# A hybrid decoder layer on one core: half of the opening's row of c by a broadcast load, the first x on ScalarE's queue, and the order planned anew

## Chip, core and metric

The kernel runs on one core of a Trainium2 chip. The metric is the device time of one execution in microseconds (us), shown as the median of several runs. A profiled execution has a time of its own, and its span runs from the first instruction to the last.

## What is computed

One layer over 1024 tokens with a model width of 1024, in f32. Cut to what matters:

```python
c_act = jax.nn.silu(c)
mod = c_act @ mod_w[l] + mod_b[l]
shift, scale, gate = jnp.split(mod, 3, axis=-1)
h = rmsnorm(x, norm_g[l]) * (1.0 + scale[:, None, :]) + shift[:, None, :]
u = h @ w_in[l]
cv, cg, cs, lx, ls = jnp.split(u, [...], axis=-1)
v = cv * jax.nn.sigmoid(cg)
v = causal_depthwise_conv(v, dw_w[l], dw_b[l])          # 31 taps
v = jax.nn.silu(layernorm(v, cln_g[l], cln_b[l])) @ pw2_w[l] + pw2_b[l]
y_conv = v * jax.nn.silu(cs)
xs = causal_depthwise_conv(lx, sc_w[l], sc_b[l])        # 4 taps
r = sigmoid(per-head xs @ wr + br);  i = sigmoid(per-head xs @ wi + bi)
a = exp(-8 r softplus(-lam))
hs = scan of h = a h + sqrt(1 - a^2) (i xs)
y_lru = hs * jax.nn.silu(ls)
x = x + (1.0 + gate[:, None, :]) * (jnp.concatenate([y_conv, y_lru], axis=-1) @ w_out[l])
return rmsnorm(x, final_g)
```

The modulation needs silu(c), a vector of 1024, multiplied into each of 3072 rows of mod_w (which the host hands over turned, so that a row lies in a partition).

## The kernel before

Data lie with channels in the 128 partitions and tokens along the free axis, so a tensor of 1024 by 1024 is eight tiles of 128 by 1024. Every f32 product is made of three passes on TensorE: an operand is cast to a shorter type ("hi", on ScalarE), the remainder ("lo") is formed by a subtraction on VectorE or GpSimd or by an accumulating DMA, and hi by hi, lo by hi and hi by lo are added in PSUM.

Stages, in order: the opening; the input products (forty column blocks of w_in, `slots`, some of them in pairs that save a part of the products, `duo`); the gates and scans of the recurrent group, whose heads are the `g` entries among the slots; the recurrent half of the output products (`lru_pair`); the layer norm of the conv group; its pointwise products (`pw2`); the other half of the output products, with the closing norm and the stores.

The opening (lines 1825 to 2032) does not wait for the norm of x. Its first products, `first`, take four column blocks of w_in and x scaled by `gs = (1 + scale) * norm_g` alone; the norm of a token is multiplied in afterwards. So the first product needs the first eighth of `gs`, which needs a dot product of silu(c) with 128 rows of mod_w. For it silu(c) must lie as a row in every partition:

- V, all the small vectors, is loaded first (line 1483); c lies in it as a column per block, 128 by 8. ScalarE makes `cs` of it (line 1834).
- TensorE spreads `cs` into a row in all partitions: per block one product of the column, broadcast along the free axis, with the identity (`spread_c`, lines 1843 to 1846). There are two halves of four blocks, each in a PSUM tile of its own, `c_row0` and `c_row1`. Each product in f32 shows as two MATMUL instructions, so sixteen in all.
- VectorE takes the dot of each half with the first block of mod_w (`first_dot`, lines 1938 to 1950). The two halves are added through the bias `b1`; then `gs` (line 1961), the scaled x `uh` (line 1973), and the first product can start.
- ScalarE copies the halves of the row to SBUF as `sc` for the later dots.

TensorE fills its time before that with idle products of ones, twelve of them (`IDLE`), four ahead of the spread and eight behind it. ScalarE also makes exp(-|lam|) there (`sp_u`, lines 1836 and 1837) and loads the table for the square root (line 1838), so that three tables are loaded one after the other in the first six microseconds.

Loads are issued by SyncE (SP) in the order of `LOADS`: the first block of mod_w ("s0"), the first weights ("w0"), the first half of x ("a0") and its second ("b0"), and then for each further block mod_w, weights and x. The first x tile comes in two halves of 256 KB, the halves of its columns (`x_load`, lines 1859 to 1866).

The order of all instructions is planned by the program itself before it emits anything (`Plan.order`, from line 1224). Each operation has an engine, an estimated cost and a priority; the planner simulates the engines and lets each take, of the operations that are ready, the one with the lowest priority number. A load is ready to be read some fixed time after its issue. The table `TURNS` adds small corrections to the priorities of single operations, some nine hundred of them. `ORDER` is the list of the column blocks and gates behind the opening.

Of the kernel before, what the change touches and what calls it, by code (L numbers as in the profile page):

```python
# [9 lines left out]
F32 = mybir.dt.float32  # L10
# [4 lines left out]
P = 128  # L15
# [19 lines left out]
ORDER = "i10 i24 i2 g0 i25 i11 i3 i26 i33 i12 i4 g1 i34 i23 g2 i13 i35 i5 i27 g3 i20 i39 i14 i6 i28+i36 i15 i30+i37 i7 i29+i38 g6 g4 g5 i31 i19 i22+i18 g7 i21"  # L35
# [55 lines left out]
KQ = 0.5  # L91
# [9 lines left out]
DENG = {14: ("POOL", "DMA", "DVE"), 17: ("POOL", "DVE", "DVE"), 20: ("DVE", "DVE", "DMA"), 21: ("DMA", "DMA", "DVE"), 24: ("DMA", "DVE", "POOL"), 26: ("DVE", "DMA", "DMA"), 27: ("POOL", "DMA", "POOL"), 30: ("DVE", "DVE", "DVE"), 35: ("DMA", "POOL", "DVE"), 36: ("POOL", "POOL", "POOL"), 39: ("DVE", "DVE", "POOL"), 40: ("DVE", "DVE", "DMA")}  # L101
# [7 lines left out]
LTP = 0.0  # L109
# [13 lines left out]
XADDP = -1.5  # L123
TSRC = "POOL"
HSP = -60
# [3 lines left out]
CENG = {21: "POOL", 17: "DVE", 36: "DVE", 33: "POOL", 22: "POOL", 15: "POOL", 16: "DVE", 27: "POOL", 20: "POOL", 31: "POOL", 34: "POOL", 24: "POOL", 29: "POOL", 38: "POOL", 39: "DVE", 32: "POOL"}  # L129
# [7 lines left out]
SQADD = -1.0  # L137
BEHIND0 = 2
# [39 lines left out]
PDIRECT = (4,)  # L178
D1S = {15: -1.35, 17: -1.35, 18: -1.35, 19: 0.0, 20: -1.35, 21: -0.3, 22: 0.0, 23: -1.35, 25: -1.35, 26: -1.35, 29: -0.3, 32: -1.35, 33: -0.3, 35: -1.35, 36: -1.35, 38: -1.35, 39: -0.3, 40: 0.0, 41: -1.35}
# [22 lines left out]
    ("ACT", "c1", "cq1_11", 0): 1.2,  # L202
    ("ACT", "c1", "cq1_12", 0): -7,
    ("ACT", "c1", "cq1_13", 0): -2.2,
    ("ACT", "c1", "cq1_14", 0): -5,
    ("ACT", "c1", "cq1_15", 0): 2,
# [5 lines left out]
    ("ACT", "c3", "c3", 0): 6.4,  # L212
    ("ACT", "c3", "cq3_1", 0): 5.6,
    ("ACT", "c3", "cq3_10", 0): 1.7,
    ("ACT", "c3", "cq3_11", 0): 5.9,
    ("ACT", "c3", "cq3_12", 0): 1.4,
    ("ACT", "c3", "cq3_13", 0): 8,
    ("ACT", "c3", "cq3_14", 0): 0.2,
    ("ACT", "c3", "cq3_2", 0): 2,
    ("ACT", "c3", "cq3_3", 0): 4.8,  # L220
    ("ACT", "c3", "cq3_4", 0): 1.4,
    ("ACT", "c3", "cq3_5", 0): 0.3,
    ("ACT", "c3", "cq3_6", 0): 3.3,
    ("ACT", "c3", "cq3_7", 0): 5.7,
    ("ACT", "c3", "cq3_8", 0): 6.7,
    ("ACT", "c3", "cq3_9", 0): 1.7,
    ("ACT", "c3", "es3", 0): 2.8,
    ("ACT", "c3", "lnsq3", 0): 0.2,
    ("ACT", "c5", "lnsq5", 0): 0.1,
    ("ACT", "c6", "caccs6", 0): -1.6,  # L230
    ("ACT", "c6", "vha3", 0): 2,
    ("ACT", "c7", "c7", 0): -0.1,
    ("ACT", "c7", "caccs7", 0): 1,
    ("ACT", "c7", "vhb3", 0): -2.3,
    ("ACT", "cacc2", "c2", 0): -0.1,
    ("ACT", "cacc6", "c6", 0): -0.7,
    ("ACT", "caccs7", "c7", 0): -0.7,
# [6 lines left out]
    ("ACT", "cr4", "cr4", 0): 7.9,  # L244
    ("ACT", "cr4", "vha2", 0): 6.4,
    ("ACT", "dn37", "wk37", 0): -1.6,
    ("ACT", "first_u0", "first_u0", 0): 8.1,
    ("ACT", "fraw2", "fhi2", 0): -1,
# [8 lines left out]
    ("ACT", "gate6_1", "g6", 0): 0.1,  # L257
    ("ACT", "graw6", "ghi6", 0): 0.1,
# [5 lines left out]
    ("ACT", "lh3", "ll3", 0): -4,  # L264
# [8 lines left out]
    ("ACT", "next5", "scs0", 0): -0.1,  # L273
    ("ACT", "ps13", "xs2", 0): 0.1,
    ("ACT", "ps17", "sls2", 0): -2,
    ("ACT", "ps18", "scs7", 0): -8,
# [3 lines left out]
    ("ACT", "psbias", "psbias", 0): -4,  # L280
# [8 lines left out]
    ("ACT", "r7", "r7", 0): -1.2,  # L289
    ("ACT", "r7", "r7", 1): -3.2,  # L290
# [3 lines left out]
    ("ACT", "raw27", "whi27", 0): 0.1,  # L294
    ("ACT", "raw34", "whi34", 0): -0.1,
    ("ACT", "raw35", "whi35", 0): -0.1,
    ("ACT", "raw36", "whi36", 0): -2.4,
    ("ACT", "raw38", "whi38", 0): -0.1,
# [4 lines left out]
    ("ACT", "rawout0_1", "h34out0", 0): 1.9,  # L303
    ("ACT", "rawout0_1", "hlout0", 0): 2,
    ("ACT", "rawpw20_1", "h34pw20", 0): 0.1,
    ("ACT", "rawpw21_0", "whipw21", 0): 0.7,
    ("ACT", "rawpw22_1", "h34pw22", 0): 1,
# [24 lines left out]
    ("ACT", "v1", "cq1_9", 0): -1,  # L332
# [12 lines left out]
    ("ACT", "v3", "cq3_1", 0): 1.6,  # L345
# [5 lines left out]
    ("ACT", "v3", "cq3_4", 0): 1.8,  # L351
    ("ACT", "v3", "cq3_5", 0): -0.1,
    ("ACT", "v3", "cq3_6", 0): 1.8,
# [10 lines left out]
    ("ACT", "vt1", "vhc1", 0): -0.1,  # L364
# [4 lines left out]
    ("ACT", "whi32", "wlo32", 0): -0.1,  # L369
    ("ACT", "whipw20", "wlopw20", 0): -2,  # L370
    ("ACT", "wz37", "wsh37", 0): -1.9,
    ("ACT", "x0", "uh0", 1): -0.1,
    ("ACT", "x2", "uh2", 0): 4,
    ("ACT", "x3", "uh3", 2): -0.9,
    ("ACT", "x4", "uh4", 2): 0.1,
# [7 lines left out]
    ("ACT", "x7", "uh7", 1): 0.3,  # L383
    ("ACT", "xpw2_1", "yc2", 1): -0.3,
    ("ACT", "xs4", "xsh4", 0): 0.1,
# [6 lines left out]
    ("ACT", "yh4", "yl4", 0): -5.7,  # L392
    ("ACT", "yhc0", "ylc0", 0): 0.9,
    ("ACT", "yhc1", "ylc1", 0): 1,
# [7 lines left out]
    ("DVE", "a1", "r1", 1): 0.4,  # L402
    ("DVE", "a4", "r4", 1): 1,
    ("DVE", "a6", "r6", 1): 0.3,
    ("DVE", "a7", "r7", 0): -0.1,
    ("DVE", "acc0", "lp0", 1): -0.3,
# [13 lines left out]
    ("DVE", "c2", "caccs2", 11): -0.1,  # L420
# [11 lines left out]
    ("DVE", "c4", "caccs4", 8): 0.1,  # L432
# [3 lines left out]
    ("DVE", "c4", "caccs4", 13): -0.2,  # L436
# [11 lines left out]
    ("DVE", "c5", "caccs5", 12): -0.2,  # L448
    ("DVE", "c5", "caccs5", 13): -0.1,
    ("DVE", "c5", "caccs5", 14): 2.9,  # L450
    ("DVE", "c5", "caccs5", 15): -3.8,
    ("DVE", "c5", "caccs5", 16): 1.3,
    ("DVE", "c5", "lnwide", 0): -0.5,
    ("DVE", "c5", "mean", 0): -1.5,
    ("DVE", "c5", "vlb2", 0): 2.1,
    ("DVE", "c5", "vt2", 1): 1.6,
    ("DVE", "c5", "vu2", 0): 8.9,
    ("DVE", "c6", "cacc6", 0): -0.6,
    ("DVE", "c6", "caccs6", 2): 1,
    ("DVE", "c6", "caccs6", 4): -0.5,  # L460
    ("DVE", "c6", "caccs6", 6): 2,
# [2624 lines left out]
```

## Time and profile before

| | |
|---|---|
| runs shown | 721.14, 722.94, 723.27 us; median 722.94 us |
| the profiled execution | 722.46 us, of which the span is 720.6 us |
| TensorE busy | 710.4 us, 99% of the span |
| VectorE busy | 641.5 us, 89% |
| ScalarE busy | 477.3 us, 66% |
| GpSimd busy | 218.2 us, 30% |
| granted TensorE clock, mean | 0.997 |
| moved by DMA | 137.53 MB, 191 GB/s |

In the rows that follow, PE is TensorE's matrix multiply, DVE VectorE, ACT ScalarE, POOL GpSimd and SPq the queue of SyncE. A row of the timeline gives the start in us from the span's start, the duration in us, engine, line, operation, the tiles written and read (buffer numbers left out), the shape and the count; in brackets stands the engine's idle time before it and what ended that. A row of a wait gives the engine with the tile, what it waited for, the total in us, how often, and the longest. Times of matmuls are start to end, and matmuls overlap, so that the distance between starts is what one costs.

### The profile page before, as it was taken

The page shows a single profiled execution, that of the slowest core. Times are in us where ns is not written, and L with a number is a line of the kernel's source. Part 1 is how long each engine was busy: PE and PEld are TensorE (multiplying, and loading weights), DVE is VectorE, ACT ScalarE, POOL GpSimd, SP SyncE. Part 2 cuts the span into 40 slices and gives each one's busy share as a digit, 9 for nine tenths or more (in the row PEclk, how much of TensorE's full clock was granted, in tenths as well). Part 3 has the DMA queues.
Part 4 walks back from the last instruction along what each step waited for, and adds up shares of the span by engine and source line. Part 5 has one row for each costly group of instructions (what it writes and reads, how often), then busy time and mean ns, then how long its engine had stood idle before and what let it go on. Part 6 is the DMA issues. An engine that isn't in the chain of part 4 may idle for free.

```text
span 720.6 us, 9035 instructions
## 1 busy us (share of the span) xinstructions
PE 710.4 (99%) x3230; PEld 590.3 (82%) x3230; DVE 641.5 (89%) x885; ACT 477.3 (66%) x604; POOL 218.2 (30%) x188
## 2 busy tenths in 40 slices
PE   9999999999999999999999999999999999999995
PEld 8888888888888888888888888887887888878885
DVE  7989999799999989969988998998589976998747
ACT  7651598847857874974794979937589653744422
POOL 0022434543676752474162351100102100100001
PEclk9999999999999999999999999999999999999998
DMA  9935458999697999699664339999638755892006
GB/s 341 407 154 176 73 149 204 246 270 204 119 253 187 250 240 229 169 230 206 211 176 117 88 98 282 264 301 246 161 81 204 183 124 123 239 279 93 27 1 233
DMA packets 45500, 137.53 MB, mean 191 GB/s; under 512 B 5144, under 2 KB 14624, under 8 KB 45344
## 3 DMA queue, kind: packets, MB, share of 16 engines
q0 software_dynamic: 16848, 45.52, 35.2%
q1 hardware_dynamic: 27600, 90.53, 35.1%
q10 hardware_dynamic: 1008, 0.92, 0.4%
q8 instruction: 25, 0.41, 0.2%
q14 instruction: 19, 0.16, 0.1%
HBM read 84.22 MB, written 25.69 MB: 153 GB/s over the span
## 4 chain that ended last, share of the span: by engine, by line
PE 78%; DVE 10%; ACT 4%; issue 4%; DMA 3%; POOL 1%; DVEq 0%; POOLq 0%; ACTq 0%
PE ps L1575 34%; PE xpw L1751 6%; PE xout L1751 6%; PE first L1884 5%; PE dn L2713 3%; PE ypw L1751 3%; PE gate L2315 3%; PE dn L1575 3%; DVE caccs L1434 2%; PE up L1575 2%; PE lx L2468 2%; PE y L1721 1%; DMA wlo<-in_w_out_dram 1%; DMA wloout<-in_w_out_dram 1%; PE zpw L1751 1%
## 5 line engine op out<-in xcount | busy, mean ns | idle before, releaser
L1575 PE MATMUL ps<-uh,whi 128*128 128x512 f32 x448 | 138.0, 389 | 0.0
L1575 PE MATMUL ps<-uh,wlo 128*128 128x512 f32 x448 | 137.9, 389 | 0.0
L1575 PE MATMUL ps<-ul,whi 128*128 128x512 f32 x448 | 137.9, 389 | 0.0
L1575 PEld LDWEIGHTS ps<-uh,wlo 128*128 128x128 f32 x448 | 84.1, 188 | 17.5
L1575 PEld LDWEIGHTS ps<-ul,whi 128*128 128x128 f32 x448 | 84.1, 188 | 17.4
L1575 PEld LDWEIGHTS ps<-uh,whi 128*128 128x128 f32 x448 | 84.0, 188 | 17.4
L1434 DVE SCALAR_TENSOR_TENSOR cacc<-v,V,cacc 128x511 f32<-128x511 f32 (+14 forms) x90 | 66.5, 739 | 0.3
L1434 DVE SCALAR_TENSOR_TENSOR caccs<-v,V,caccs 128x511 f32<-128x511 f32 (+6 forms) x84 | 62.4, 743 | 1.0
L1434 DVE SCALAR_TENSOR_TENSOR caccs<-c,wsum,caccs 128x511 f32<-128x511 f32 (+6 forms) x84 | 62.2, 740 | 0.8
L1415 ACT CAST whi<-raw 128x1024 fp32r<-128x1024 f32 (+1 forms) x44 | 44.1, 1006 | 26.7 <-issue 14.0
L1423 ACT ACT_TABLE_LOAD x46 | 59.0, 1283 | 3.2 <-DVE r L2327 1.1
L1442 POOL TENSOR_TENSOR wlo<-raw,whi 128x1024 fp32r<-128x1024 f32 (+1 forms) x15 | 36.4, 2428 | 75.5 <-ACT whi L1415 73.5
L1447 POOL DMA_DIRECT2D es<-cq x30 | 28.3, 943 | 32.1 <-DMA es<-cq 11.1
L1434 DVE SCALAR_TENSOR_TENSOR modw<-modw,sc 128x1024 f32<-128x1024 f32 x23 | 32.7, 1425 | 0.0
L1442 DVE TENSOR_TENSOR wlo<-raw,whi 128x1024 fp32r<-128x1024 f32 (+1 forms) x22 | 30.7, 1395 | 0.6 <-ACT whi L1415 0.6
L1447 POOL DMA_DIRECT2D oo<-co x26 | 26.5, 1054 | 11.1 <-issue 5.5
L1423 ACT ACTIVATE uh<-x,shift 128x512 fp32r<-128x512 f32 x16 | 10.5, 713 | 23.9 <-PE ps L1575 23.9
L1442 POOL TENSOR_TENSOR o<-fin,bc 128x256 f32<-128x256 f32 (+1 forms) x6 | 4.9, 831 | 70.8 <-ACT bc L1415 70.8
L1447 POOL DMA_DIRECT2D accd<-acc x8 | 7.3, 914 | 62.1 <-ACT acc L1423 44.2
L1423 ACT ACTIVATE finsq<-fin 128x512 f32<-128x512 f32 (+2 forms) x14 | 7.9, 570 | 27.0 <-DVE fin L1434 15.1
L1423 ACT ACTIVATE cq<-v,V 128x511 f32<-128x511 f32 (+14 forms) x30 | 21.0, 707 | 6.5 <-DVE r L2327 3.1
L1447 POOL DMA_DIRECT2D lz<-in_w_out_dram x16 | 14.4, 987 | 34.4 <-ACT lz L1423 30.5
(525 smaller groups left out, 1937.8 us busy)
## 6 DMA issues: line engine op xcount, KB each, us to landing
raw<-in_w_in_dram SPq DMA_DIRECT2D x36, 512.0 KB, 4.6
modw<-in_mod_w_dram SPq DMA_DIRECT2D x24, 512.0 KB, 7.6
scsd<-scs SPq DMA_DIRECT2D x8, 512.0 KB, 3.9
raw<-in_w_out_dram SPq DMA_DIRECT2D x8, 512.0 KB, 4.5
accd<-acc POOLq DMA_DIRECT2D x8, 512.0 KB, 8.0
rawpw<-in_pw_dram SPq DMA_DIRECT2D x8, 512.0 KB, 3.9
scsr<-scsd SPq DMA_DIRECT2D x8, 512.0 KB, 4.3
rawout<-in_w_out_dram SPq DMA_DIRECT2D x8, 512.0 KB, 4.4
```

The lines of the kernel that those rows point to most:

```text
L1415: act.copy(out(), in_())
L1423: act.activation(out=out(), in_=in_(), func=func, **kw)
L1434: dve.scalar_tensor_tensor(out=out(), in0=in0(), scalar=scalar, in1=in1(), op0=op0, op1=op1, accum_out=accum)
L1442: lambda: e.tensor_tensor(out=out(), in0=a(), in1=b(), op=op), prio, r, w,
L1447: return S.op("POOL", ISSUE, lambda: pool.dma_start(out(), a(), accum_op=ALU.add), prio, r, w, lag=RATE * n / T, after=after, flight=flight)
L1575: pe.matmul(ps()[:, a - off:b - off], k3(lhs)()[:, at, :], rhs[k]()[:, a:b], start=(k == first and lhs is wh and rhs is xh and (a - off) % ...
L1721: pe.matmul(to(), half(*lhs)()[:, j * P:j * P + P], half(*rhs)()[:, c0:c1], start=a == "S1" and j == 0 and t == 0, stop=j == KT // 2 - 1 a ...
L1751: pe.matmul(half(ps, 0)(), half(*lhs)()[:, j * P:j * P + P], half(*rhs)(), start=start and at == 0 and i == 0, stop=at == len(order) - 1 a ...
L1884: pe.matmul(ps()[:, a - off:b - off], fw_part(lhs, k, i * P, i * P + P)(), rhs()[:, a:b], start=k == 0 and lhs is wh and rhs is xh, stop=k ...
L2315: pe.matmul(ps()[:, c0:c1], lhs()[:, j, :], rhs()[:, c0:c1], start=st == 0, stop=st == 2)
L2468: pe.matmul(half(ps, h)(), lhs()[:, o:o + P], half(*rhs)(), start=begin and at == 0 and t == 0, stop=at == len(order) - 1 and t == len(ter ...
L2713: pe.matmul(half(ps, h)(), lhs()[:, o:o + P], half(rhs, z)(), start=begin and j == 0 and t == 0, stop=j == NJ - 1 and t == 2, skip_group_c ...
```

## The change

In the opening:

- The column of c is loaded by itself, ahead of V, and `cs` is made of it.
- Only the first half of the row is spread by TensorE, four blocks instead of eight, into one PSUM tile. The second half comes as a new input, `c_half`, by a load that broadcasts 512 values to all partitions, issued on SP ahead of the first block of mod_w; ScalarE applies silu to it in place.
- The first dot takes the loaded half, the second the spread half. One copy to SBUF is left.
- exp(-|lam|) is made behind the silu of the loaded half, and the table for the square root is loaded behind the seventh scaled x.
- The first half of the first x tile is issued by ScalarE and not by SP.
- The idle products read one column of ones, broadcast, and not a full tile.

In the planner's inputs: two pairs of neighbours in `ORDER` change places (g6 with g4; g7 with i21), the priorities `KQ` (the casts of the pairs' sums), `LTP` (the sums of the recurrent group) and some others change, and several hundred entries of `TURNS` are new, gone or different. The entries of `DENG`, `CENG` and `D1S` count only at the numbers of pairs (27, 30, 33, 37); at those only an entry that equals the default is added. The output lies in memory as 128 rows of 8192 values, and the host puts it back; a store still writes rows of 1 or 2 KB. `SQE` and `OPAIR` are empty.

```diff
-ORDER = "... i29+i38 g6 g4 g5 i31 i19 i22+i18 g7 i21"
+ORDER = "... i29+i38 g4 g6 g5 i31 i19 i22+i18 i21 g7"
...
-KQ = 0.5
+KQ = -0.3
...
-LTP = 0.0
+LTP = -0.5
...
+CRP, EXPP, SQK, SCP = -100.6, -100.3, 6, -98.9
...
+    c_col = const.tile([P, KT], F32, tag="c_col", name="c_col")
+    sp.dma_start(c_col, vecs[:, OFF["c"]:OFF["c"] + KT])
     V = const.tile([P, NVEC], F32, tag="V", name="V")
     sp.dma_start(V[:, :DWW], vecs[:, :DWW])
...
+    one = const.tile([P, 1], F32, tag="one", name="one")
+    dve.memset(one, 1.0)
...
-    cs, ps_c = ctile("cs", KT), [mm_tile(f"c_row{z}") for z in (0, 1)]
-    ACT(-130, lambda: cs, lambda: V[:, OFF["c"]:OFF["c"] + KT], AF.Silu, KT, w=[("cs", 0)])
+    cs, ps_c = ctile("cs", KT), mm_tile("c_row")
+    ACT(-130, lambda: cs, lambda: c_col, AF.Silu, KT, w=[("cs", 0)])
     sp_u = S.buf("sp_u", "sp_u")
-    ACT(-129, sp_u, lambda: V[:, OFF["lam"]:OFF["lam"] + KT], AF.Abs, KT, w=[sp_u])
-    ACT(-128, sp_u, sp_u, AF.Exp, KT, scale=-1.0, r=[sp_u, ("cs", 0)], w=[sp_u])
-    ACT(-127, lambda: junk, lambda: eps_t, AF.Sqrt, 1, r=[sp_u], w=[("junk", 0)])
...
-        pe.matmul(psb()[:, :P], ones, ones, start=True, stop=True)
...
+        pe.matmul(psb()[:, :P], one.to_broadcast([P, P]), one.to_broadcast([P, P]), start=True, stop=True)
+
+    def spread_c():
+        for k in range(KT // 2):
+            pe.matmul(ps_c()[:, k * P:k * P + P], cs[:, k:k + 1].to_broadcast([P, P]), ident,
                       start=True, stop=True)
...
+        elif z == 0:
+            S.op("ACT", 0.05, lambda: act.dma_start(half(t, z)(), xT[:P // 2, :].rearrange(
+                "r (h f) -> (r h) f", h=2)), -140, [], halves(t, 0, H), moved=0.73)
...
+    DMA(CRP, half(sc, 1), lambda: c_half.to_broadcast([P, H]), FULL_BYTES // 2, w=[(sc, 1)])
+    silu_row = ACT(CRP, half(sc, 1), half(sc, 1), AF.Silu, H, r=[(sc, 1)], w=[(sc, 1)])
+    ACT(EXPP, sp_u, lambda: V[:, OFF["lam"]:OFF["lam"] + KT], AF.Abs, KT, w=[sp_u], after=[silu_row])
+    ACT(EXPP, sp_u, sp_u, AF.Exp, KT, scale=-1.0, r=[sp_u, ("cs", 0)], w=[sp_u])
...
-        parts = ((0, H, a0, ("a0", 0)), (H, T, col(macc, j), ("macc", j)))
-        for z, (a, e, to, key) in enumerate(parts):
-            o = STT(p, part(m, a, e), part(m, a, e), 1.0, half(ps_c[z], 0), ALU.mult, ALU.mult, H,
-                accum=to, r=[(m, z), ps_c[z]], w=[(m, z), key])
-            ACT(-101, half(sc, z), half(ps_c[z], 0), "copy", H, r=[ps_c[z]], w=[(sc, z)],
-                after=[o])
-            if z == 0:
+        for z, to, key in ((1, a0, ("a0", 0)), (0, col(macc, j), ("macc", j))):
+            row, rk = (half(sc, 1), (sc, 1)) if z else (half(ps_c, 0), (ps_c, 0))
+            m_ = part(m, z * H, z * H + H)
+            o = STT(p, m_, m_, 1.0, row, ALU.mult, ALU.mult, H, accum=to, r=[(m, z), rk], w=[(m, z), key],
+                    after=[] if z else [o])
+            if z:
                 S.op("DVE", 0.2, lambda: dve.tensor_tensor(
                     out=col(b1, 0), in0=a0, in1=col(b1, 0), op=ALU.add), p,
                     [("a0", 0), ("b1", 0)], [("b1", 0)], lock=True)
+        ACT(SCP, half(sc, 0), half(ps_c, 0), "copy", H, r=[(ps_c, 0)], w=[(sc, 0)], after=[o])
...
+        if k == SQK:
+            ACT(p, lambda: junk, lambda: eps_t, AF.Sqrt, 1, r=[sp_u], w=[("junk", 0)], after=[o])
```

More of the change, by code (lines that the diff above doesn't have):

```diff
@@ L517 @@
     ("DVE", "lnss", "lnsq5", 0): -1,
+    ("DVE", "lx1", "ld1", 0): 0.1,
     ("DVE", "lx3", "ld3", 0): -1,
@@ L1810, in rstd @@
                       after=after if k == 0 else [])
-            for _ in range(warm[k] if warm else 0):
+            for _ in range(warm[k] if k < len(warm) else 0):
                 S.op("PE", 0.22, warm_mm, prio, [], [idle], after=[at], columns=4 * P)
```

529 lines of the change are left out of this document (260 added, 269 removed).

## The prediction

> **What bounds the kernel now.** I read the page's engine table first, then the chain of waits, then what TensorE waited for, then the opening instruction by instruction.
>
> ```profile
> span 720.6 us, 9035 instructions
> PE 710.4 (99%) x3230; PEld 590.3 (82%) x3230; DVE 641.5 (89%) x885; ACT 477.3 (66%) x604; POOL 218.2 (30%) x188
> ```
>
> TensorE (PE) is busy for 710.4 of 720.6 us. "Busy" is modelled, so I check it against the chain, where groups of matmuls stand with their counts:
>
> ```profile
> 3.14 3.63 PE c_row L1845 x16
> 6.77 1.90 PE token_stats L1841 x16
> 8.67 32.68 PE first L1884 x144
> ```
>
> The 144 matmuls of `first` take 32.68 us, 0.227 us each, with no gap. So the kernel is TensorE work end to end, with a head before the first product, a few waits, and a tail of scaling and stores after the last product. What TensorE waited for:
>
> ```profile
> PE lw L1575 <- DMA wlo<-in_w_out_dram: 0.8, 1, 0.8
> PE zout L1751 <- DMA wloout<-in_w_out_dram: 0.6, 1, 0.6
> PE finbc L1798 <- ACT finsqz L1423: 0.3, 1, 0.3
> PE xpw L1751 <- ACT vha L1415: 0.2, 1, 0.2
> ```
>
> One more wait is hidden in a pair of matmuls of the recurrent group's first products:
>
> ```profile
> 466.62 1.03 PE L2468 MATMUL ly<-yls,lsh 128*128 128x512 f32 x2
> 467.49 0.40 PE L1575 MATMUL dn<-uh,whi 128*128 128x512 f32 x1
> ```
>
> Two matmuls that should take 0.45 us hold the engine for 0.87 (466.62 to 467.49): 0.4 us lost. Everything that a new order can win inside is thus 0.8 + 0.6 + 0.2 + 0.4 = 2.0 us; the 0.3 belongs to the closing norm. The rest must come from the head.
>
> The head, in the timeline of the opening:
>
> ```profile
> 0.74 1.28 ACT L1423 ACT_TABLE_LOAD   x1 [0.74 <-PEq L3078]
> 0.75 0.39 SPq L1483 DMA_DIRECT2D V<-in_vecs_dram  x1
> 1.06 2.07 PE L1841 MATMUL token_stats<-ones 128*128 128x128 f32 x8 [1.06 <-DVE ones L1492]
> 1.20 0.42 SPq L1461 DMA_DIRECT2D modw<-in_mod_w_dram  x1
> 2.13 0.91 SPq L1461 DMA_DIRECT2D x<-in_xT_dram  x2
> 2.67 0.21 ACT L1423 ACTIVATE cs<-V 128x8 f32<-128x8 f32 x1 [0.64 <-DMA V<-in_vecs_dram]
> 3.02 3.75 PE L1845 MATMUL c_row<-ident,cs 128*128 128x128 f32 x16
> 5.10 0.69 DVE L1434 SCALAR_TENSOR_TENSOR modw<-modw,c_row 128x512 f32<-128x512 f32 x1 [2.19 <-PE c_row L1845]
> 5.83 0.16 DVE L1948 TENSOR_TENSOR b<-a,b 128x1 f32<-128x1 f32 x1
> 6.38 0.62 ACT L1415 CAST fhi<-fraw 128x512 fp32r<-128x512 f32 x1
> 6.56 2.11 PE L1841 MATMUL token_stats<-ones 128*128 128x128 f32 x16
> 6.81 0.69 DVE L1434 SCALAR_TENSOR_TENSOR modw<-modw,c_row 128x512 f32<-128x512 f32 x1 [0.82 <-PE c_row L1845]
> 7.54 0.22 DVE L1961 SCALAR_TENSOR_TENSOR gs<-macc,b,V 128x1 f32<-128x1 f32 x1
> 7.79 0.49 DVE L1456 TENSOR_SCALAR uh<-x,gs 128x512 fp32r<-128x512 f32 x1
> 8.43 1.17 PE L1884 MATMUL first<-uh,fhi 128*128 128x512 f32 x4
> ```
>
> The chain is V landing, silu of c (2.67), sixteen spread matmuls (3.02 to 6.77), two half dot products on VectorE (5.10 and 6.81, both released by `c_row`), `gs`, `uh`, first product at 8.43. The second dot could have started right behind the add, at 5.83 + 0.16 = 5.99; it waited 0.82 us for the second half of the spread.
>
> **The change part by part.** The spread matmuls fall from sixteen to eight. That takes 1.9 us (8 x 3.75/16) from TensorE's opening, but none of it was product work, and the eight idle matmul pairs behind them still stand in the queue. With dots back to back, the first product follows the start of the first dot by 5.99 - 5.10 = 0.9 and then by 8.43 - 6.81 = 1.62: 2.5 us. If the first dot still began at 5.10, the first product would come at 7.6, a gain of 0.8. But what the first dot now waits for is no longer `c_row`; it is the block of mod_w, and the row's half with its silu. These come from transfers:
>
> ```profile
> modw<-in_mod_w_dram SPq DMA_DIRECT2D x1, 512.0 KB, 3.6
> modw<-in_mod_w_dram SPq DMA_DIRECT2D x24, 512.0 KB, 7.6
> lnwide<-lnrow SPq DMA_DIRECT2D x1, 512.0 KB, 5.8
> 0.00:3.00 3.00, 1.94 (x8) 1.79 (x9) 0.77 (x5) 1.60 (x4) 0.70 (x6) 1.00 0.37 116
> 3.00:6.00 3.00, 3.00 (x15) 3.00 (x15) 0.85 (x3) 2.96 (x5) 0.00 (x0) 1.00 0.91 296
> 9.00:12.00 3.00, 3.00 (x15) 2.46 (x14) 3.00 (x6) 1.80 (x3) 0.00 (x0) 1.00 1.03 420
> ```
>
> (The first three: KB and median us from issue to landing, the first of them for the opening's first block alone; the last three end in the DMA engines' busy share and GB/s.) Before, mod_w lands at 1.20 + 3.6 = 4.8, just ahead of 5.10. After, SP issues the c column, V and the broadcast half ahead of it; SP's issues stand 0.46 us apart (0.75, 1.20), so mod_w is issued at 2.13 and, with the same 3.6 us, lands at 5.7. By bytes: V, x's first half, the broadcast and mod_w are 1,122 kB, where before V and mod_w were 598 kB. The windows moved 348 kB by 3.0 us and then 296 GB/s, so 598 kB are through at 3.85, and landing is told 0.95 later. 1,122 kB are through at 5.6: landing at 6.55, the **upper end**. At 420 GB/s behind 3.0, and with the x half (262 kB, 0.6 us at that rate) hidden in the slow first window, it is 3.0 + 1.84 + 0.95 - 0.6 = 5.2, the **lower end**. I take the issue's 5.7, which lies between. First product: 5.7 + 2.5 = 8.2, a gain of **0.2 us** (0.7 won to 0.65 lost).
>
> A page of the Trainium skill speaks against the move of x: "DMA: Bandwidth & Descriptors", "Issuing engines are not separate DMA queues", says that transfers started from several engines share the same 16 DMA engines, so that only issue time is saved. By that rule alone the upper end holds and the opening loses 0.65; no run here has yet shown a transfer from ScalarE in the opening.
>
> The broadcast reads one row 128 times. The trace has one like it, `lnwide<-lnrow`: 512 KB in 5.8 us, between the 3.6 and the 7.6 of the mod_w blocks of that size, so I price it as ordinary. By bytes the half row lands where mod_w did, 4.8, and its silu (0.6 us, as the cast of 128x512) is done at 5.5, under cover of mod_w's 5.7. Queued behind it on ScalarE stand the exp table (1.28), Abs and Exp (0.2 each, as `cs`) and then `fhi`: done at 5.5 + 1.7 + 0.62 = 7.8, against 8.2 where it is needed. The cover is 0.4 us; if the row is later than that, `fhi` sets the start. x issued by ScalarE ahead of its table load costs nothing: 0.4 (as SP's issues) + 1.28 from 0.74 ends at 2.4, before the c column lands (V's 2.67 or a little sooner). The sqrt table load moves behind k = 6, where ScalarE has room.
>
> Next along: 256 KB more (0.6 us at 420 GB/s) stand ahead of the second block.
>
> ```profile
> 11.27 0.22 DVE L1961 SCALAR_TENSOR_TENSOR gs<-macc,b,V 128x1 f32<-128x1 f32 x1
> 11.52 1.34 ACT L1423 ACTIVATE uh<-x,gs 128x512 fp32r<-128x512 f32 x2 [1.18 <-DVE gs L1961]
> 13.31 0.39 PE L1884 MATMUL first<-uh,fhi 128*128 128x512 f32 x1
> ```
>
> Its first half `uh` is ready near 11.52 + 0.67 = 12.2 and used from about 13.3; 0.6 later still fits a start 0.2 earlier, with 0.3 to spare.
>
> The planner's part: LTP from 0.0 to -0.5 puts the recurrent group's sums ahead of other VectorE work, and those sums (`yls`) are what the 0.4 us at 466.62 waited for. I count that 0.4 as won (0 to 0.4). The transfers behind the waits of 0.8 and 0.6 are touched only by small priorities; I leave both. In ORDER, g7 and i21 change places, which needs a look:
>
> ```profile
> 441.24 0.62 PE L2315 MATMUL gate<-xsh,ghi 128*128 128x512 f32 x2
> 462.59 0.87 POOL L1447 DMA_DIRECT2D yl<-sls  x1 [4.75 <-ACT yl L1423]
> yl<-sls POOLq DMA_DIRECT2D x1, 512.0 KB, 6.6
> 471.36 0.61 PE L1575 MATMUL lp<-yl,whi 128*128 128x512 f32 x2
> 474.08 0.61 PE L1575 MATMUL lp<-yl,whi 128*128 128x512 f32 x2
> ```
>
> Head 7's gate at 441.24 leads to its `yl` landing at 462.59 + 6.6 = 469.2; `lp` reads it at 471.36 at the earliest and at 474.08 at the latest (the first and the last of three such groups; the rows don't tell the heads apart). i21 is 48 matmuls, 10.9 us. I take 0 for the swap in the sum, since the same matmuls of i21 now fill the gaps that the gate filled, and the pair has other products that do not read head 7; the other end is the rival below. The table entries for slot numbers that are no pair, the new layout of the output (rows of the same length) and the new unused options cost nothing.
>
> The sum, against the profiled execution's own 722.46 (span 720.6 and 1.9 around it): 722.46 - 0.2 - 0.4 = **721.9**. That execution is 0.5 below the median of the runs shown, 722.94.
>
> **The rivals.** *The waits go too*: the new order clears 0.8, 0.6 and 0.2 as well, and the opening is at its best: 722.46 - 2.0 - 0.7 = 719.8. For it: the waits are isolated, each on one late transfer or cast. Against: a new order can make new ones as easily. *Head 7 late*: with g7 behind i21, `yl` is 10.9 us later, less the slack of 2.1 to 4.8: 6.1 to 8.8 us of wait in the first pair if nothing else can be drawn forward, 0 if all can; with half of the larger, 4.0, and no gain at `yls`, 722.46 - 0.2 + 4.0 = 726.3, slower. It decides when the gate's second half runs more than 4.8 us later than 441.24 without other products of the pair going ahead. *The opening does not do what it says*: mod_w at 6.55 or the row's silu behind it puts the first product at 9.1: 722.46 + 0.65 = 723.1.
>
> The skill's "TensorE: Matmul & The Clock Gate", Part 1, says that the clock rises after some 3.4 us of work, on a window that runs free of the kernel. The trace agrees that it rises (idle matmuls take 0.26 us at 1.06, 0.13 at 6.56). In an execution where it rose before the spread, the second half would not have held the dots, and the change would win nothing there: that is the third rival again.
>
> **How the numbers follow.** Forecast 0.58, waits gone 0.21, head 7 late 0.12, opening worse 0.09. The bound of 0.3% is 2.2 us, about what a measurement of this kernel can tell from no change. Against 722.94, the forecast and the third rival lie within it, the first lies past 720.8, the second past 725.1: faster 0.21, same 0.67, slower 0.12. The range reaches to the waits-gone case less the closing norm's 0.3 (719.5) and part of the way to head 7 late (724.6, a wait of 2.3); what lies outside is most of head 7 late and the edge of the first rival. The likeliest's own is 721.4 (opening at its best) to 723.1 (at its worst, and `yls` unchanged).
>
> **What would show it.** Right: dots back to back, the first released by a transfer of mod_w, first product between 7.7 and 8.5; no 0.87 us pair on `yls`. Wrong: the first dot waiting for the row's silu, a gap among the `first` matmuls near 13 us, or waits of `lp`, `lx` or `ly` for `yl` of several us. What would make the forecast wrong is waits of more than 2 us, new or gone, in the recurrent or output stages.

## The result and the profile after

The changed kernel takes 726.95 us in the median of nine runs (724.36 to 730.14), the kernel before, on the same chip, 722.07 (720.84 to 726.23). The ratio is 1.0061, with a 95% interval of 1.0039 to 1.0082: it is slower by 0.6%, and the prediction (721.9, no change) was wrong. (Ratios here are estimated from all the runs of both kernels and are not the quotient of the two medians.) The profiled execution took 728.77 us. From its page, the span and TensorE's row:

```profile
span 727.0 us, 9030 instructions
PE 712.1 (98%) x3222; PEld 591.5 (81%) x3222; DVE 643.4 (88%) x886; ACT 477.0 (66%) x604; POOL 217.7 (30%) x188
```

The span is 6.4 us longer than before. TensorE's busy time grew by 1.7, although the opening has eight spread products less (1.9 us): TensorE stands still for longer, and for part of the time it works more slowly. What it waited for in the changed kernel (total, times, longest):

```profile
PE zout L1740 <- DMA wloout<-in_w_out_dram: 2.3, 1, 2.3
PE first L1870 <- DVE uh L1441: 2.1, 1, 2.1
PE lw L1564 <- DMA wlo<-in_w_out_dram: 1.0, 1, 1.0
...
PE dn L2705 <- DVE dn L1427: 0.7, 1, 0.7
```

Before, the first of these was 0.6, the second was not there, the third 0.8, the fourth not there. The two large ones lie at the two ends of the kernel, one in the part that was rebuilt (the opening), one in a part that only the planner touched. The opening of the changed kernel, in the timeline:

```profile
2.13 0.43 SPq L1446 DMA_DIRECT2D modw<-in_mod_w_dram  x1
...
3.41 0.21 ACT L1408 ACTIVATE cs<-c_col 128x8 f32<-128x8 f32 x1 [0.95 <-DMA c_col<-in_vecs_dram]
...
6.05 0.63 ACT L1408 ACTIVATE sc<-sc 128x512 f32<-128x512 f32 x1 [2.43 <-DMA sc<-in_c_half_dram]
...
7.85 0.69 DVE L1419 SCALAR_TENSOR_TENSOR modw<-modw,sc 128x512 f32<-128x512 f32 x1 [3.69 <-DMA modw<-in_mod_w_dram]
...
8.44 0.62 ACT L1400 CAST fhi<-fraw 128x512 fp32r<-128x512 f32 x1
...
8.66 0.68 DVE L1419 SCALAR_TENSOR_TENSOR modw<-modw,c_row 128x512 f32<-128x512 f32 x1
...
9.64 0.49 DVE L1441 TENSOR_SCALAR uh<-x,gs 128x512 fp32r<-128x512 f32 x1
...
10.27 1.10 PE L1870 MATMUL first<-uh,fhi 128*128 128x512 f32 x2 [2.07 <-DVE uh L1441]
```

The chain has the shape that was meant: the two dots stand back to back (7.85 and 8.66), released by a transfer of mod_w. But the transfer is late, and the first product starts at 10.27, where before it started at 8.43. The loads issued in the first 2.5 us (KB, median us from issue to landing):

```profile
modw<-in_mod_w_dram SPq DMA_DIRECT2D x1, 512.0 KB, 5.6
x<-in_xT_dram ACTq DMA_DIRECT2D x1, 256.0 KB, 3.0
sc<-in_c_half_dram SPq DMA_DIRECT2D x1, 256.0 KB, 4.4
```

mod_w lands at 2.13 + 5.6 = 7.7; before it was 4.8. Four windows of the same trace (us; busy us of PE, PEld, DVE, ACT, POOL with counts; granted clock; DMA share; GB/s) show a second cost, behind each of the two waits:

```profile
10.30:13.70 3.40, 3.40 (x8) 2.66 (x9) 3.40 (x7) 2.08 (x4) 0.00 (x0) 0.51 1.03 412
14.00:17.40 3.40, 3.40 (x16) 2.81 (x15) 3.37 (x9) 2.68 (x5) 0.00 (x0) 1.00 1.03 410
645.50:648.20 2.70, 0.40 (x3) 0.02 (x1) 2.70 (x5) 0.41 (x1) 0.00 (x0) 1.00 1.08 244
648.50:652.00 3.50, 3.50 (x10) 2.69 (x9) 1.74 (x3) 1.04 (x1) 0.00 (x0) 0.52 0.77 300
```

For 3.4 us behind the wait TensorE had half its clock (the first and the fourth window, 0.51 and 0.52): 8 matmuls start where 16 start in the window after. The chain of work shows the same as a length (start, us), and the other late transfer:

```profile
10.27 34.49 PE first L1870 x144
...
637.14 11.00 DMA wloout<-in_w_out_dram
```

The 144 products of `first` took 34.49 us from the first product. Before, the chain counts them from 8.67, where the idle products end; from the first product, at 8.43, they took 32.92.

The balance of these two executions: the first product +1.8 (10.27 - 8.43), half the clock behind it +1.6 (34.49 - 32.92), the wait for wloout +1.7 (2.3 - 0.6), half the clock behind that some +1.6 (eight matmuls that each cost 0.2 more), the waits for `dn` and `wlo` +0.9 (0.7, and 1.0 - 0.8), less the 0.4 at `yls` and the 0.2 at `xpw`, which are gone. That makes 7.0, against 6.4 of the span; the 0.6 between them is not accounted for. Half the clock is not in every execution: the mean granted clock was 0.992 to 0.994 in five of the nine runs of the changed kernel, which took 726.0 to 730.1 us, and 0.996 to 0.998 in the other four, which took 724.4 to 728.0. In the 91 runs of the kernel before that stand beside the experiments it was never below 0.995. One thing went as planned, the first products of the recurrent group:

```profile
470.66 0.62 PE L2460 MATMUL ly<-yls,lsh 128*128 128x512 f32 x2
471.12 0.39 PE L1564 MATMUL dn<-uh,whi 128*128 128x512 f32 x1
```

The pair on `yls` holds the engine for 0.46 us; it was 0.87.

### The profile page after: what moved, and what is told of

It reads as the page before. It is cut to its first block, busy times and chain, and to the rows that moved or that the text cites. A ratio compares the mean times of both kernels' runs of the same rounds, so it can differ in the third digit from the quotient of the medians.

```text
span 727.0 us, 9030 instructions
## 1 busy us (share of the span) xinstructions
PE 712.1 (98%) x3222; PEld 591.5 (81%) x3222; DVE 643.4 (88%) x886; ACT 477.0 (66%) x604; POOL 217.7 (30%) x188
## 4 chain that ended last, share of the span: by engine, by line
PE 82%; DVE 8%; DMA 4%; issue 3%; POOL 1%; ACT 0%; SPq 0%; DVEq 0%; POOLq 0%
PE ps L1564 34%; PE xout L1740 6%; PE first L1870 6%; PE xpw L1740 5%; PE dn L2705 3%; PE dn L1564 3%; DVE caccs L1419 3%; PE lx L2460 3%; PE ypw L1740 3%; PE gate L2307 3%; PE up L1564 2%; DVE cacc L1419 2%; DMA wloout<-in_w_out_dram 2%; PE zpw L1740 1%; PE lx L1564 1%
## 5 line engine op out<-in xcount | busy, mean ns | idle before, releaser
L1419 DVE SCALAR_TENSOR_TENSOR modw<-modw,sc 128x1024 f32<-128x1024 f32 (+1 forms) x24 | 32.3, 1351 | 3.7 <-DMA modw<-in_mod_w_dram 3.7
L1408 ACT ACTIVATE uh<-x,shift 128x512 fp32r<-128x512 f32 x16 | 10.5, 713 | 23.9 <-PE ps L1564 23.9
L1870 PE MATMUL first<-uh,fhi 128*128 128x512 f32 x56 | 21.7, 412 | 2.1 <-DVE uh L1441 2.1
```

What stands on the lines that cost most here:

```text
L1408: act.activation(out=out(), in_=in_(), func=func, **kw)
L1419: dve.scalar_tensor_tensor(out=out(), in0=in0(), scalar=scalar, in1=in1(), op0=op0, op1=op1, accum_out=accum)
L1870: pe.matmul(ps()[:, a - off:b - off], fw_part(lhs, k, i * P, i * P + P)(), rhs()[:, a:b], start=k == 0 and lhs is wh and rhs is xh, stop=k ...
```

## Experiments

### The two parts, one at a time

`e_open` is the kernel before with the changed opening; `e_plan` is the changed kernel with the opening of before, so that only the order and the layout of the output are new.

```diff
 e_open:  before.py + hunks of the opening (c_col, c_half, spread_c, x_load, first_dot, sp_u)
 e_plan:  after.py  - the same hunks
```

> The kernel before with the changed opening alone; the engines' order behind it is that of before. If the opening is the cause: the first product starts near 10.3 us as in the changed kernel (8.4 before), the clock falls in 9 to 12 us, and the time is 3 to 5 us above before. If the new order is the cause: within 1 us of before.

> The changed kernel with the opening of before: new order, new layout of the output. If the opening is the cause: the first product at 8.4 us, and the time within 1 us of before; the wait of 2.3 us for wloout falls back below 1. If the new order is the cause: 2 us or more above before, with the wait for wloout at 2.3.

Measured: `e_open` 1.0035 (1.0011 to 1.0058), `e_plan` 1.0019 (1.0003 to 1.0035). Both parts cost, some 2.5 and 1.4 us, each less than its expectation said (3 to 5, and 2 or more), and together they make about the 1.0061 of the whole. In the chain of `e_open`, the first products:

```profile
9.71 32.89 PE first L1886 x144
```

They start 1.3 late and then run at full speed: this execution has no stretch of half clock. The waits of `e_plan`:

```profile
PE zout L1736 <- DMA wloout<-in_w_out_dram: 1.9, 1, 1.9
PE lw L1560 <- DMA wlo<-in_w_out_dram: 1.8, 1, 1.8
```

The wait for wloout belongs to the new order and not to the opening; in `e_open` it is 0.7. The 1.8 for wlo is of this execution; in the others with the new order it is 0.3 to 1.5.

### The order: one entry

Most of the order is the same in both kernels. Around the wait for wloout, the POOL queue's issues in the kernel before,

```profile
629.33 0.87 POOL L1447 DMA_DIRECT2D ylc<-yt  x1 [3.98 <-ACT ylc L1423]
634.12 0.86 POOL L1447 DMA_DIRECT2D wloout<-in_w_out_dram  x1 [3.93 <-ACT wloout L1423]
```

and in `e_plan`:

```profile
632.12 0.86 POOL L1432 DMA_DIRECT2D ylc<-yt  x1 [4.93 <-ACT ylc L1408]
635.75 0.86 POOL L1432 DMA_DIRECT2D wloout<-in_w_out_dram  x1 [2.77 <-ACT wloout L1408]
```

The 512 KB of `ylc` went out 4.8 us ahead of wloout, now 3.6. In ScalarE's order the cast `yhc` now goes ahead of the remainder `ylc` that the transfer waits for. That follows from one entry of `TURNS`, and three kernels try it: taken back in the changed kernel (`e_ylc`), taken back in `e_plan` (`e_planylc`), and put alone into the kernel before (`e_ylcb`).

```diff
 e_ylc, e_planylc:
-    ("ACT", "yhc1", "ylc1", 0): 3,
+    ("ACT", "yhc1", "ylc1", 0): 1,
 e_ylcb (in before.py):
-    ("ACT", "yhc1", "ylc1", 0): 1,
+    ("ACT", "yhc1", "ylc1", 0): 3,
```

> The changed kernel with one planner entry put back, so that on ScalarE the rest ylc of the convolution group is again written before the next cast yhc, not behind it; nothing else in any engine's order differs. Theory: in the changed order ylc is issued 0.94 us later on POOL's queue, just ahead of the second load of wloout, and that is what lets TensorE's wait of 0.6 us for wloout grow to 1.9 to 2.3. Then the wait falls to 0.5 to 1.2 us, the stretch of half clock behind it goes, and the time is 1 to 3 us below that of the changed kernel. Rival: the wait comes from the transfers of this stage as a whole (rows in DRAM, the earlier delays): it stays at 1.9 to 2.3 us and the time stays that of the changed kernel.

> The opening of before with the new order, in which the entry of ylc is put back. Theory: without the late ylc the new order costs nothing: the wait for wloout is 0.3 to 1.0 us, those for yls and xpw stay gone, against small new ones at the gates and at dn; the time is within 1 us of the kernel before, ratio 0.998 to 1.001. Rival: the rest of the new order (dn, the gates, wlo) costs 1 to 2 us by itself: ratio 1.0015 or more, as the new order with the late ylc had.

> The kernel before with only the one planner entry of the change at ylc (1 to 3), so that on ScalarE the cast yhc goes ahead of the rest ylc; nothing else differs. Theory: this swap alone makes the second load of wloout late: TensorE's wait for it grows from 0.6 us to 1.6 to 2.3, the time by 1 to 1.7 us, or by some 3 where the clock is halved behind the wait. Rival: in the order of before there is room and the wait stays under 1.0 us.

Measured: `e_ylc` 1.0038 (1.0021 to 1.0055), which is what the opening costs alone. `e_planylc` 0.9992 (0.9972 to 1.0011): the new order without this entry, and with the new layout of the output, is not measurably slower than the old one. `e_ylcb` 1.0041 (1.0019 to 1.0062): the entry alone makes the kernel before 3 us slower. The waits for wloout in the three, each from the kernel's own view of waits, in this order:

```profile
PE zout L1740 <- DMA wloout<-in_w_out_dram: 0.3, 1, 0.3
```

```profile
PE zout L1736 <- DMA wloout<-in_w_out_dram: 0.4, 1, 0.4
```

```profile
PE zout L1751 <- DMA wloout<-in_w_out_dram: 2.8, 1, 2.8
```

All three go the theory's way; `e_ylc` falls below its 0.5 and `e_ylcb` goes beyond its 2.3. There the transfers issued from 622 to 642 us show how it comes about:

```profile
ylc<-yt POOLq DMA_DIRECT2D x1, 512.0 KB, 11.3
wloout<-in_w_out_dram POOLq DMA_DIRECT2D x1, 512.0 KB, 11.4
```

In the kernel before these two take 8.5 and 9.2 us. Brought 1.0 us closer together (issued at 631.54 and 635.37), both take longer, and the second is the one that TensorE waits for. The small waits of the new order (`dn` 0.6, the gates 0.5 and 0.3 in `e_planylc`) are together more than the 0.6 that it saves at `yls` and `xpw`; the time does not show it within its interval.

### The opening: why mod_w is late

First the two things that looked new: the broadcast source, replaced by 128 equal rows in memory (`e_full`), and the idle stretch, filled with ten more idle products (`e_idle`).

```diff
 e_full:
-    DMA(CRP, half(sc, 1), lambda: c_half.to_broadcast([P, H]), ...)
+    DMA(CRP, half(sc, 1), lambda: c_half, ...)
 e_idle:
-        S.op("PE", 0.22, idle_mm, ...)
+        S.op("PE", 0.22, idle_mm if i < IDLE - 1 else lambda: [idle_mm() for _ in range(11)], ...)
```

> The changed kernel with the half row handed in as 128 equal rows, so that each partition reads a row of its own; same bytes, same place in the queue. If 128 reads of one row are what holds mod_w back: the half row lands by 4.8 us (6.0 now), mod_w by 6.5 (7.75 now), the first product by 9.1 (10.3 now), and the time is 1 to 3 us below the changed kernel. If the added bytes or ScalarE's queue do it: mod_w still at 7.5 or later and no gain over 0.5 us.

> The changed kernel with ten more idle products behind the spread, so that TensorE is busy until about 10.2 us and not idle from 8.0 to 10.3. If the idle stretch makes the clock fall: the first products stand 0.227 us apart and not 0.427, and the time is about 1.5 us below the changed kernel. If the fall has another cause: they stay at 0.427 and the time does not move by more than 0.5 us.

Measured: `e_full` 1.0054 (1.0027 to 1.0082). Its first loads:

```profile
modw<-in_mod_w_dram SPq DMA_DIRECT2D x1, 512.0 KB, 5.6
...
sc<-in_c_half_dram SPq DMA_DIRECT2D x1, 256.0 KB, 2.9
```

The half row lands at 1.65 + 2.9 = 4.5 and not at 6.0, so the broadcast itself is slow; but in this execution mod_w lands as late as with it. `e_idle` 1.0066 (1.0043 to 1.009): in the profile the products start at 10.06 straight behind the idle ones and run at full clock, and the time is no shorter than that of the changed kernel. A gain of 1.5 us would be 0.2%, no more than either interval is uncertain by, so the run does not rule it out. Half a clock at the start comes in some executions only (`e_open` and `e_full` have none there either).

Then the places in the queue: x back on SP (`e_xsp`); mod_w issued ahead of the half row (`e_modw`); the same with full rows (`e_modwf`).

```diff
 e_xsp:
-        elif z == 0:
-            S.op("ACT", 0.05, lambda: act.dma_start(half(t, z)(), xT[:P // 2, :]...
 e_modw, e_modwf:
-    DMA(CRP, half(sc, 1), ...)
+    DMA(-99.7, half(sc, 1), ...)          # e_modwf: with the full rows of e_full
```

> The changed kernel with the first half of x back on SP's queue behind the first weights; c's column, the half row and the order of the rest stay. Theory (what is ahead of mod_w in bytes holds it back): 262 kB less are ahead of mod_w, at the 420 GB/s of the later windows 0.6 us; mod_w lands near 7.0 instead of 7.7 and the first product starts near 9.6. Rival (mod_w's own first packets are slow, whatever is ahead of it): mod_w lands at 7.5 or later and the first product starts at 10.0 or later.

> The changed kernel with SP issuing mod_w ahead of the broadcast half row of c, not behind it. Theory (place in the queue): mod_w is issued 0.47 us earlier and 262 kB are no longer ahead of it: it lands at 6.2 to 6.7 instead of 7.7, the half row 0.7 to 1.5 us behind it, so that with its silu the first product starts at 9.6 to 10.3: no gain, because the other operand is now the late one. Rival (slow first packets): mod_w lands at 7.2 or later also with nothing but V, the column and x ahead of it.

> The changed kernel with SP issuing mod_w ahead of the half row, and the half row as 128 equal rows; the column load and x on ScalarE's queue stay. Theory (broadcast slow, x and the column cost some 0.7 us): mod_w lands near 5.2, the half row near 5.9 to 7.0 (a stretch of slow transfers falls into 4 to 6.5 us in every run), the first dot starts at 6.5 to 7.7 and the first product at 9.0 to 10.0. Rival (x on ScalarE's queue and the column are what makes the opening late): the half row lands past 7.5 and the first product starts past 10.2 also with full rows.

Measured: 1.0072 (1.0045 to 1.0099), 1.0081 (1.0054 to 1.0107) and 1.0078 (1.0053 to 1.0103); no single one of these is measurably faster than the changed kernel. In `e_xsp` mod_w lands at 7.5 and the first product starts at 10.10, as its rival said: x on ScalarE's queue is not the main thing at mod_w. The loads of `e_modw`,

```profile
modw<-in_mod_w_dram SPq DMA_DIRECT2D x1, 512.0 KB, 3.6
...
sc<-in_c_half_dram SPq DMA_DIRECT2D x1, 256.0 KB, 6.3
```

and of `e_modwf`:

```profile
modw<-in_mod_w_dram SPq DMA_DIRECT2D x1, 512.0 KB, 5.2
...
sc<-in_c_half_dram SPq DMA_DIRECT2D x1, 256.0 KB, 5.4
```

With mod_w ahead, `e_modw` has it at 5.2, sooner than its theory and its rival, with the 3.6 us of before; now the broadcast row is the late one, at 8.4, and the first product comes at 11.56, later than the theory's 10.3. `e_modwf` came out as its rival (half row at 7.5, first product at 10.67): here mod_w took 5.2 us and landed at 6.8, with the same transfers ahead of it as in `e_modw`. Landings in this stretch thus differ by 1.6 us between two executions, and one of them alone proves little.

### The opening mended, and its parts put back

`e_mend` undoes what may make the loads late and keeps the idea: no column load, x on SP, V then mod_w then the half row in full rows, the spread half in the first dot and the loaded half in the second, the exp back at the start; the entry of `ylc` is taken back too. Four kernels put one thing back each.

```diff
 e_mend:
-CRP, EXPP, SQK, SCP = -100.6, -100.3, 6, -98.9
+CRP, EXPP, SQK, SCP = -99.7, -129.0, 6, -98.5
-    sp.dma_start(c_col, vecs[:, OFF["c"]:OFF["c"] + KT])
-    ACT(-130, lambda: cs, lambda: c_col, AF.Silu, ...)
+    ACT(-130, lambda: cs, lambda: V[:, OFF["c"]:OFF["c"] + KT], AF.Silu, ...)
-        for z, to, key in ((1, a0, ("a0", 0)), (0, col(macc, j), ("macc", j))):
+        for z, to, key in ((0, a0, ("a0", 0)), (1, col(macc, j), ("macc", j))):
 e_mendb: the half row by to_broadcast again
 e_mendr: the half row issued ahead of mod_w again (-100.6)
 e_mendc: c_col loaded ahead of V again
 e_menda: x's first half issued by ScalarE again
```

> Both parts of the change mended: c's column comes with V as before, SP issues V, then mod_w, then the half row of c (128 equal rows, no broadcast), and x keeps its old place on SP; the first dot uses the half that TensorE spreads, the second the loaded half; the exp stays at the start as before and ScalarE's table of silu is loaded again behind it; the planner entry of ylc is put back, the rest of the changed order stays. Theory: mod_w lands near 4.8 as before, the half row near 5.4 to 6.0, its silu is done at 6.4 to 6.6, the second dot starts there instead of 6.81, first product 8.0 to 8.3 (before 8.43); the wait for wloout is 0.5 to 1.2, the waits of 0.4 for yls and 0.2 at xpw stay gone: 0.5 to 1.0 us below the kernel before, ratio 0.998 to 1.000, which a measurement can hardly tell from none. Rival: the half row lands as late as 7.0 also here and the first product starts past 9.0, so that the time is above the kernel before.

> The mended kernel with the half row of c read by the broadcast load again, in the same place of SP's queue behind mod_w; nothing else differs. Theory (the broadcast itself is slow: it took 1.8 to 3.2 us in the kernels that have it, full rows 0.64 and 0.69): mod_w still lands near 4.6, the half row at 6.5 to 7.8 instead of 5.2, the second dot waits for its silu, and the first product starts at 9.2 to 10.3 instead of 8.1; the time is 1 to 2 us above the mended kernel. Rival (the place in the queue is all that counts): the half row lands by 5.6 and the first product starts by 8.4.

> The mended kernel with SP issuing the half row of c (full rows) ahead of mod_w and not behind it; nothing else of weight differs. Theory (place: what stands ahead of mod_w in bytes makes it late): 336 kB instead of 74 are ahead of it; it lands 0.7 us or more later than in the mended kernel, at 5.2 to 6.2 instead of 4.5, and the first product starts at 8.5 to 9.3. Rival (place does not matter much, only the broadcast and x on ScalarE's queue do): mod_w by 5.0, first product by 8.3.

> The mended kernel with c's column loaded by itself ahead of V, as the changed kernel does; nothing else differs. Theory: SP's first issue is spent on 4 kB, so V, mod_w and the half row land 0.5 to 0.7 us later (mod_w 5.0 to 5.3) and the column itself no sooner than V did (2.4 to 2.7): first product 8.6 to 9.0. Rival: the column lands by 2.0 and the other loads no later: first product by 8.2.

> The mended kernel with the first half of x issued by ScalarE at its start. The planner's order behind the opening comes out another way with it, so only the opening is to be read. Theory: x's 262 kB share the transfer engines with mod_w: mod_w and the half row land 0.6 to 0.9 us later than in the mended kernel (5.1 to 5.5 and 5.8 to 6.5), ScalarE's table load ends 0.4 later, first product 8.5 to 9.1. Rival: the transfers from ScalarE's queue fill the slow first 3 us: mod_w by 4.8, first product by 8.3.

Measured: `e_mend` 721.87 us against 722.6 of before in the same runs, ratio 1.0003 (0.998 to 1.0026): the loss is gone, and nothing that can be measured is won. Its opening:

```profile
5.13 0.69 DVE L1419 SCALAR_TENSOR_TENSOR modw<-modw,c_row 128x512 f32<-128x512 f32 x1 [2.19 <-PE c_row L1828]
...
6.49 0.69 DVE L1419 SCALAR_TENSOR_TENSOR modw<-modw,sc 128x512 f32<-128x512 f32 x1 [0.47 <-ACT sc L1408]
...
8.11 1.17 PE L1865 MATMUL first<-uh,fhi 128*128 128x512 f32 x4 [0.60 <-DVE uh L1441]
```

The second dot starts 0.3 sooner than before (6.81), and so does the first product (8.43). Its loads:

```profile
modw<-in_mod_w_dram SPq DMA_DIRECT2D x1, 512.0 KB, 3.3
sc<-in_c_half_dram SPq DMA_DIRECT2D x1, 256.0 KB, 3.6
```

mod_w at 4.5, the half row at 5.2. Now the parts. `e_mendb`, with the broadcast, has

```profile
sc<-in_c_half_dram SPq DMA_DIRECT2D x1, 256.0 KB, 5.4
```

the half row at 7.0, 1.8 later, and the first product at 9.39, both as its theory said. Its mod_w lands at 5.4 and not near 4.6, although the same lies ahead of it as in `e_mend`. Its ratio of 1.0011 (0.9985 to 1.0036) can't be told from that of `e_mend`; the 1 to 2 us of its theory are not measured. `e_mendr`, with the row ahead of mod_w, has

```profile
modw<-in_mod_w_dram SPq DMA_DIRECT2D x1, 512.0 KB, 4.0
```

mod_w at 1.65 + 4.0 = 5.6, 1.1 later, inside the theory's 5.2 to 6.2; but the first product starts at 8.16, against the theory's 8.5 to 9.3, because the silu of the loaded half ends at 6.4 in either order (it stands behind the exp's tables) and the second dot starts at 6.5 in both. Ratio 1.0002 (0.9987 to 1.0018). `e_mendc` has mod_w at 5.2, 0.6 later, and the first product as much later, from the chain:

```profile
8.77 32.92 PE first L1867 x144
```

with a ratio of 1.0004 (0.9985 to 1.0023). It is not mod_w that delays the product there: the second dot waits for the silu of the half row until 6.97 (6.49 in `e_mend`), and `uh` then 0.21 for x. `e_menda` does not compute the layer, so that its time says nothing and only its opening is read. V and mod_w land later:

```profile
modw<-in_mod_w_dram SPq DMA_DIRECT2D x1, 512.0 KB, 3.9
...
V<-in_vecs_dram SPq DMA_DIRECT2D x1, 72.0 KB, 2.8
```

mod_w at 5.1, 0.6 later, and V at 3.6, 0.9 later than in `e_mend`, with the spread behind it; the first product at 9.06.

A landing is an issue plus a time from the issue. The issue is sure: the column and the half row each take one place of SP's queue ahead of mod_w, 0.46 us, and together they move its issue from 1.20 to 2.13. The time from the issue scatters. With V alone ahead it was 3.2 to 4.2 us in six executions (`before`, `e_plan`, `e_ylcb`, `e_planylc`, `e_mend`, `e_mendb`), and none of the parts put back alone is outside that: 4.0 with the row, 3.5 with the column, 3.9 with x. With all of them it was 5.1 to 5.9 in four (the changed kernel, `e_open`, `e_idle`, `e_ylc`), so that mod_w landed at 7.2 to 8.0 and not at 4.4 to 5.4. That the parts together make it late is shown; how this second share, of about 2 us, divides among them is not: without x on ScalarE's queue it is still 5.4 (`e_xsp`), with full rows still 5.6 (`e_full`).

What x on ScalarE's queue does to the loads at the head of SP's queue is shown: V took 2.7 to 2.8 us from its issue in the eight executions with it and 1.9 to 2.1 in the nine without.

Neither `e_mend` nor `e_planylc` (721.81 against 722.85) can be told from the kernel before; no version here beats it by more than its measurement is uncertain.

## Why the prediction was wrong, step by step

**The chain behind the first dot: right.** 2.5 us from the first dot to the first product were forecast; it is 10.27 - 7.85 = 2.4. The dots stand back to back, mod_w releases the first, the silu of the row and the exp's table load stay under cover, `fhi` is done at 9.06, a microsecond before `uh` is. No gap near 13 us.

**When mod_w lands: wrong, and this is the step that failed in the opening.** The prediction took "the issue's 5.7", from the 3.6 us that mod_w needed before, and as the upper end 6.55 by bytes. It landed at 7.7. The 3.6 belongs to a transfer with 74 kB ahead of it; in the new queue 602 kB are ahead, and the time from the issue became 5.6. The upper end counted the bytes rightly but took the rates of before, 116 GB/s to 3 us and 296 from there on. The changed kernel moved 73 GB/s in its first 3 us and then

```profile
3.00:6.00 3.00, 2.24 (x11) 2.27 (x11) 0.25 (x2) 0.21 (x1) 0.00 (x0) 1.00 0.90 188
6.00:9.00 3.00, 2.20 (x16) 2.01 (x14) 1.11 (x4) 2.78 (x5) 0.00 (x0) 1.00 0.99 395
```

By these rates the prediction's own count gives 219 kB by 3 us, 783 by 6 and 1,122 at 6.9, and with its 0.95 to the landing 7.8, where 7.7 was measured. So the term that failed is the rate: a queue with other loads in it did not move its bytes as the old one did. Why it moved so few between 3 and 6 us stays open.

A row of the kernel before that hints at it was not read, in the loads issued in its first 9 us:

```profile
x<-in_xT_dram SPq DMA_DIRECT2D x2, 256.0 KB, 5.2
```

The first of these two halves was the 1,122nd kB of before and was issued at 2.13, the very count and time that the prediction worked out for mod_w. The 5.2 is told for the second half alone, issued near 2.6, which landed at 7.8; of the first the row tells no landing, and the trace's own signals for it end at 7.10. Both are later than the prediction's count by bytes has them (6.55 for the first, 7.45 for the second). With mod_w at 7.1 the first product comes at 9.6.

**The column of c "at V's 2.67 or a little sooner": wrong.** `cs` ran at 3.41. Without x on ScalarE's queue the column lands at 2.4 to 2.6 (`e_mendc`, `e_xsp`), only 0.2 before V does in `e_mend`, and it takes the first place of SP's queue from V and mod_w. With x there it lands at 3.1 to 3.5 in seven executions, and V goes from 2.7 to 3.6 in `e_menda`. The prediction priced x on ScalarE at its issue, and for its lower end hid the bytes in the slow first window.

A page of the Trainium skill, "DMA: Bandwidth & Descriptors", in "Issuing engines are not separate DMA queues", says that starting transfers from several engines saves issue time only, since they share the engines. The prediction named it; V's 0.9 us in `e_menda` agree with it.

**The broadcast "priced as ordinary": wrong.** The half row was forecast at 4.8 and landed at 6.0; in the same place full rows are 1.5 (`e_full`) and 1.8 us (`e_mend` beside `e_mendb`) sooner, and 0.9 (`e_modwf` beside `e_modw`) even where mod_w ahead of them came 1.6 later. The likeness with `lnwide`, which reads 512 KB in 5.8 us elsewhere, said nothing on a queue that everything waits for.

**The idle stretch in front of the first product: not in the prediction.** TensorE stood idle for 2.1 us, and in this execution lost 1.6 more at half its clock. The prediction used the clock only for how it rises. It read that rise out of idle products of 0.26 and 0.13 us, while the granted clock in its own rows is 1.00 from 0 to 6 us; the two readings of that trace differ, and no run settles which is right.

**The waits of 0.8 and 0.6 "touched only by small priorities; I leave both": wrong, the step that failed in the planner's part.** One of these small priorities moved a 512 KB transfer by 1.0 to 1.2 us against its neighbour on POOL's queue and made 0.6 into 1.9 to 2.8. It alone is worth 0.4% (`e_ylcb`). The prediction's list of what would be wrong, "waits of more than 2 us, new or gone, in the recurrent or output stages", names the place, but no rival priced it.

**`yls` 0.4 won, g7 with i21 nothing: right.** The pair on `yls` is whole again, the 0.2 at `xpw` went too; no product waits for head 7's `yl`. That it was `LTP` that freed `yls` was not tried by itself. From 425 to 480 us the order of TensorE's instructions is the same as before, with tile numbers left out, so *Head 7 late* had nothing to stand on. (Its sum takes "half of the larger, 4.0"; half of 8.8 is 4.4.)

**The rivals.** *The opening does not do what it says* was the nearest, with its sign and its place, but at 0.65 us; it is 1.3 in `e_open` and 1.8 in the profile. The forecast and *The waits go too* both rested on the one landing time.

## What to carry to other kernels

Price a transfer that is moved by its new issue and by the landing time of whatever stood in its new place before, and not by its own old duration; and take rates of an old queue as a guess only. In a kernel that is one engine's work end to end, look at every wait of half a microsecond and ask which transfers run beside it: an entry that swaps two casts of 1 us cost as much as a new opening. And when several small things are changed ahead of one critical load, put them back one at a time, each in several executions: with the same transfers ahead, one load's time from its issue differed by up to 1.6 us here, more than any single part seemed to cost.

## What the runs showed of the hardware

- **Half a clock after a wait of 2 us.** In the profiles shown here (without `e_menda`), TensorE's waits before the first product or for wloout of 1.8 us or less were never followed by a stretch of half clock; of thirteen waits of 1.9 to 3.5 us nine were, for 3.4 us, in which some 1.6 are lost (34.49 against 32.92 for `first`). The four without it lasted 1.9, 1.9, 2.4 and 2.6. In `e_ylcb` the clock fell about 1.5 us after work had started again. The Trainium skill's "TensorE: Matmul & The Clock Gate", Part 1, has the window of 3.4 us and a fall after an idle window of that length; the length of the slow stretch agrees, but here less idle time than a window was enough.
- **A broadcast load is slow on a short queue.** 256 KB from one row of memory landed 1.5 and 1.8 us later than the same from 128 rows, in the same place. Behind the column and V the broadcast landed at 5.7 to 6.5 in five executions, full rows at 4.5 in one.
- **Two large transfers on POOL's queue, a microsecond closer.** `ylc` and wloout, 512 KB each, took 8.5 and 9.2 us when issued 4.8 us apart, 10.5 and 10.6 at 3.6 (`e_plan`), 11.3 and 11.4 at 3.8 (`e_ylcb`).
- **The first transfers are slow, and by how much depends on the queue.** From 9 us on the DMA engines moved 410 to 420 GB/s in the kernels before and after; from 3 to 6 us they moved 296 before and 188 after, and in `e_menda`, with x on ScalarE's queue and the full rows behind mod_w, 409. Why, the runs don't show.
